# Which operand stands still: q/k/v, query and up products with stationary weights in a two-layer decoder trunk

## The chip, the core and the metric

The program runs on one core of a Trainium2 chip, in one launch, on fp32 inputs in device memory. The metric is the device time of one execution in microseconds (us), compared by the median of several runs. The engines are TensorE (PE in the profile; its weight loads have a row of their own, PEld), VectorE (DVE), ScalarE (ACT), GpSimd (POOL) and SyncE (SP), which issues the weight loads from device memory. Each engine takes its instructions in order from its own queue and waits for the others by semaphores. "The slices" are the profile's 40 equal parts of the span.

## The reference

Two layers over one sequence of 256 rows of 2048. Layer 0 is a gated DeltaNet, layer 1 a differential attention; each is followed by a squared-ReLU MLP of width 8192, and a LayerNorm closes every sub-layer.

```python
def gated_deltanet(x, w_in, ...):                    # w_in: 2048 x (q 2048 | k 2048 | v 2048 | z 2048 | 32)
    p = x @ w_in
    qkv = causal_conv_silu(p[..., :GDN_CONV_CH], conv_w)
    z = ...; beta = sigmoid(b); g = -exp(a_log) * softplus(a + dt_bias)
    # q, k normalised per head of 128; chunked delta rule with a triangular solve
    o = rms_norm(o, norm_w, GDN_EPS) * jax.nn.silu(z)
    return o @ w_out

def diff_attention(x, w_q, ...):                     # k, v = x @ w_kv
    attn = softmax(q1 k1) - lam * softmax(q2 k2)     # per head, causal
    return (rms_norm(attn @ v) * (1.0 - lambda_init)) @ w_o

def sq_relu_mlp(x, w_up, w_down):
    return jnp.square(jax.nn.relu(x @ w_up)) @ w_down

x = layer_norm(ALPHA * x + h, ln_g[l, 0], ln_b[l, 0])
x = layer_norm(ALPHA * x + sq_relu_mlp(x, mlp_w_up[l], mlp_w_down[l]), ln_g[l, 1], ln_b[l, 1])
```

## The kernel before

**Split products.** Every large product keeps fp32 accuracy by splitting both operands into two parts of the type fp32r: hi, a copy by ACT (L78), and lo, the rest, a subtraction by DVE (L79). A product is then x_hi W_hi + x_hi W_lo + x_lo W_hi, summed in PSUM. `xhl` holds both parts of x with features on the 128 partitions, as blocks of [part, row tile t, feature block k, 128 rows].

**A weight tile** is 128 input features by 1024 columns, 512 KB, loaded into `wr` by SP, and split into `wh` and `wl`. `product` (L166) runs 12 matmuls on it: for each of two row tiles t and two column halves g, with a 128x128 block of x as the stationary operand and 512 columns of the weights streaming past:

```python
mm(ps, xh, wh[:, c], start=(k == 0), stop=False)                      # L174
mm(ps, xh, wl[:, c], start=False, stop=False)                         # L175
self.last = mm(ps, xl, wh[:, c], start=False, stop=(k == nk - 1))     # L176
```

The result has rows on partitions, [128 rows, 512 columns], one PSUM bank for each (g, t): four accumulators `acc`, which a product of 1024 columns uses all. The other four banks, `ps`, serve everything else.

**The plan.** `gemm` puts a product on a list; `run` (L121) walks it in steps of four weight tiles (48 matmuls). A step is t = 0 for all tiles, then t = 1; the loads of the next step's tiles are written between the two. After each t, `pump(rate)` writes down the next units of other work: one from the deque `chain`, and up to `rate` from `units`. `soon` puts a function behind a tile of the next product. What is written down is what each engine's queue holds, in that order, save that TensorE's part of some functions is tied behind the last matmul so far.

**Back to features.** The next product needs its operand with features on partitions. So up products (`up`, L341) take relu and square, and then four 128x128 transpositions by TensorE (`transpose4`, L200; the matmuls stand at L204) and another split per accumulator. q, k and v of DeltaNet are copied out of `acc` by ACT (L693), transposed, and copied into a tile `raw` of [128 channels, 8 heads, 256 rows] (`channels`, L498). Differential queries and keys are turned the same way in `heads` (L787).

**DeltaNet's order.** It works in two halves of 8 heads. Each half's plan is k, q, v (1024 columns each, four steps), `rate=2`; z follows both halves. When a product is through, `follow` (L704) queues units: four conv units of two heads for k or q (`qk_unit`, L476: a causal convolution of four taps on DVE, L471, a tanh and a square on ACT, and sums of squares by matmuls of one column, L485), four `v_unit`s, and, after q, `scalars`, four `score` units (L513: masks on DVE, L525 and L526, decay matmuls at L530 to L535, k k and q k at L550 and L551, their weighting on DVE at L553 and L554) and the inverse, as a chain. The gate projection stands ahead of q of the first half (`gates`, L410): there the small weights are stationary, hi against hi and lo of x (512 columns, L425) and lo against x's hi (256 columns, L426).

**The start.** `load_x` (L226) loads x and splits it quarter by quarter, the first at once, the others as units between the steps of the first product.

In the differential part a `score` unit (L809) is one pair of heads and one row tile: matmuls (L819), a masked maximum on DVE (L830), four exponentials on ACT (L834), and the weighted difference.

## Time and profile before

| | |
|---|---|
| time, median of 3 runs | 2463.02 us (2461.49 to 2467.75) |
| the profiled execution | 2465.03 us, span 2463.3 us |
| granted TensorE clock, mean of the span | 0.992 |
| PE busy | 2416.1 us, 11492 matmuls |
| DVE busy | 1497.2 us, 2333 instructions |
| ACT busy | 1078.2 us, 1474 instructions |
| POOL busy | 90.3 us |
| matmuls at L174, L175, L176 with x as operand | 3 x 1920, with a mean of 393 to 398 ns |
| weight splits, L78 on ACT and L79 on DVE | 800 of 1052 ns, 785 of 1227 ns |

A matmul's row gives its own duration, from its start to its modelled end, and matmuls overlap: where they follow each other without a gap, the time that one costs is the distance from one start to the next. A row of a listing of instructions has its start (us from the start of the span), its duration (us), engine, line, operation, output and inputs, shapes, and in brackets, if it waited, how long and for what. A row of a group has the number of instructions, the busy time and the mean duration in ns, and the idle time before them.

### The profile page before, as it was taken

Reading aid. Unit: us, or ns where it says so; the run is one execution under the profiler, and the core shown is the slowest. Engines: PE = TensorE matmul, PEld = TensorE weight load, DVE = VectorE, ACT = ScalarE, POOL = GpSimd, SP = SyncE. Lnnn points to the kernel's source line nnn. Section 1 sums busy time; section 2 is a strip of 40 time slices with the busy share of each in tenths; the row PEclk is TensorE's granted clock in tenths of the full one; section 3 lists DMA queues with packets and bytes.
Section 4 is the critical chain, followed back from the end, with each engine's and each line's share of the span. In section 5 each row is a group of like instructions: output and inputs, shape, how many; then the busy total and the mean of one; then the engine's idle time right before and its main releaser. Section 6 shows DMA issues by size and latency. Waiting matters only on the chain.

```text
span 2463.3 us, 30465 instructions
## 1 busy us (share of the span) xinstructions
PE 2416.1 (98%) x11492; PEld 1983.3 (81%) x11492; DVE 1497.2 (61%) x2333; ACT 1078.2 (44%) x1474; POOL 90.3 (4%) x94
## 2 busy tenths in 40 slices
PE   8999999998999999999998999999999999999997
PEld 7888888887888888888887878788788888888886
DVE  4789689667554544545557575665755554555556
ACT  4545345433443433434433464643443443443442
POOL 0010010002000000000002000000200000000001
PEclk9999899999999999999999999999999999999999
DMA  6545345564555556565554545455455555656553
GB/s 229 155 139 175 98 140 160 166 233 158 188 185 191 182 194 222 172 214 182 195 197 146 180 137 171 155 174 167 161 198 195 182 190 186 217 179 214 185 195 121
DMA packets 120211, 438.84 MB, mean 178 GB/s; under 512 B 13760, under 2 KB 13792, under 8 KB 119040
## 3 DMA queue, kind: packets, MB, share of 16 engines
q1 hardware_dynamic: 115920, 420.79, 52.0%
q0 software_dynamic: 2560, 11.13, 1.4%
q10 hardware_dynamic: 1584, 4.98, 0.5%
q8 instruction: 90, 1.47, 0.2%
q14 instruction: 57, 0.47, 0.1%
HBM read 433.70 MB, written 3.15 MB: 177 GB/s over the span
## 4 chain that ended last, share of the span: by engine, by line
PE 90%; DVE 6%; DMA 2%; issue 1%; ACT 1%; POOL 0%; ACTq 0%; POOLq 0%; DVEq 0%
PE acc L174 27%; PE acc L175 27%; PE acc L176 27%; PE ps L204 3%; DVE wl L79 1%; DVE blk L266 1%; DVE blk L265 1%; PE ps L819 1%; ACT wh L78 1%; PE ps L550 1%; DMA wr<-in_gdn_w_in_dram 1%; PE ps L485 1%; DMA wr<-in_mlp_w_up_dram 0%; PE ps L621 0%; PE ps L847 0%
## 5 line engine op out<-in xcount | busy, mean ns | idle before, releaser
L79 DVE TENSOR_TENSOR wl<-wr,wh 128x1024 fp32r<-128x1024 f32 x785 | 954.5, 1227 | 675.0 <-ACT wh L78 632.1
L78 ACT CAST wh<-wr 128x1024 fp32r<-128x1024 f32 x800 | 832.1, 1052 | 945.6 <-PE acc L176 757.2
L174 PE MATMUL acc<-wh,xhl 128*128 128x512 f32 x1920 | 764.3, 398 | 0.0
L175 PE MATMUL acc<-wl,xhl 128*128 128x512 f32 x1920 | 757.7, 395 | 3.2 <-POOL wl L79 3.2
L176 PE MATMUL acc<-wh,xhl 128*128 128x512 f32 x1920 | 754.8, 393 | 0.0
L174 PE MATMUL acc<-wh,blk 128*128 128x512 f32 x1280 | 500.0, 391 | 0.0
L176 PE MATMUL acc<-wh,blk 128*128 128x512 f32 x1280 | 499.4, 390 | 0.0
L175 PE MATMUL acc<-wl,blk 128*128 128x512 f32 x1280 | 499.1, 390 | 0.0
L175 PEld LDWEIGHTS acc<-wl,xhl 128*128 128x128 f32 x1920 | 363.7, 189 | 75.7 <-POOL wl L79 4.4
L174 PEld LDWEIGHTS acc<-wh,xhl 128*128 128x128 f32 x1920 | 363.8, 189 | 73.8 <-issue 1.7
L176 PEld LDWEIGHTS acc<-wh,xhl 128*128 128x128 f32 x1920 | 362.7, 189 | 73.9
L176 PEld LDWEIGHTS acc<-wh,blk 128*128 128x128 f32 x1280 | 240.4, 188 | 50.1
L174 PEld LDWEIGHTS acc<-wh,blk 128*128 128x128 f32 x1280 | 240.4, 188 | 49.5
L175 PEld LDWEIGHTS acc<-wl,blk 128*128 128x128 f32 x1280 | 240.5, 188 | 49.2
L293 DVE SCALAR_TENSOR_TENSOR blk<-blk,acc 128x512 f32<-128x512 f32 x80 | 54.7, 685 | 85.2 <-PE acc L176 85.2
L204 PE MATMUL ps<-ident,sm 128*128 128x128 f32 x512 | 81.3, 275 | 2.5 <-DVE sm L869 1.8
L204 PEld LDWEIGHTS ps<-ident,sm 128*128 128x128 f32 x512 | 61.3, 140 | 27.3 <-PE acc L176 7.1
L78 ACT CAST blk<-ps 128x512 fp32r<-128x512 f32 x80 | 46.8, 585 | 70.9 <-PE ps L204 70.9
L347 DVE TENSOR_TENSOR sm<-sm 128x512 f32<-128x512 f32 x64 | 44.0, 691 | 52.6 <-ACT sm L346 52.2
L79 DVE TENSOR_TENSOR blk<-ps,blk 128x512 fp32r<-128x512 f32 x80 | 55.0, 688 | 30.1 <-ACT blk L78 30.1
L346 ACT ACTIVATE sm<-acc 128x512 f32<-128x512 f32 x64 | 38.2, 597 | 65.4 <-PE acc L176 62.4
L471 DVE SCALAR_TENSOR_TENSOR sm<-blk,g_cw,sm 128x255 f32<-128x255 f32 (+2 forms) x144 | 60.8, 474 | 0.0
(202 smaller groups left out, 1049.7 us busy)
## 6 DMA issues: line engine op xcount, KB each, us to landing
wr<-in_mlp_w_up_dram SPq DMA_DIRECT2D x256, 512.0 KB, 4.7
wr<-in_mlp_w_down_dram SPq DMA_DIRECT2D x256, 512.0 KB, 5.2
wr<-in_gdn_w_in_dram SPq DMA_DIRECT2D x128, 512.0 KB, 4.4
wr<-in_shared_w_kv_dram SPq DMA_DIRECT2D x64, 512.0 KB, 5.1
wr<-in_gdn_w_out_dram SPq DMA_DIRECT2D x32, 512.0 KB, 5.4
wr<-in_diff_w_q_dram SPq DMA_DIRECT2D x32, 512.0 KB, 4.6
wr<-in_diff_w_o_dram SPq DMA_DIRECT2D x32, 512.0 KB, 4.7
blk<-in_ln_g_dram POOLq DMA_DIRECT2D x4, 1024.0 KB, 7.2
```

The lines of the kernel that those rows point to most:

```text
L78: self.nc.scalar.copy(hi, src)
L79: (engine or self.nc.vector).tensor_tensor(lo, src, hi.bitcast(F32), op=ALU.subtract)
L174: mm(ps, xh, wh[:, c], start=(k == 0), stop=False)
L175: mm(ps, xh, wl[:, c], start=False, stop=False)
L176: self.last = mm(ps, xl, wh[:, c], start=False, stop=(k == nk - 1))
L204: self.nc.tensor.transpose(pt[:, i], src[:, i * P : (i + 1) * P], self.ident)
L265: v.scalar_tensor_tensor(xc, xc, ln["mv", t][:, 0:1], ln["g"][:, c], op0=ALU.subtract, op1=ALU.mult)
L266: v.scalar_tensor_tensor(xc, xc, ln["rs", t], ln["b"][:, c], op0=ALU.mult, op1=ALU.add)
L293: self.nc.vector.scalar_tensor_tensor(rc, rc, alpha, ps, op0=ALU.mult, op1=ALU.add)
L346: self.nc.scalar.activation(a, ps, AF.Relu)
L347: self.nc.vector.tensor_tensor(a, a, a, op=ALU.mult)
L471: v_.scalar_tensor_tensor(y[:, i, d:], u[:, : T - d], w(j), y[:, i, d:], op0=ALU.mult, op1=ALU.add)
```

## The change

In the products q, k and v of DeltaNet, the queries and the second half of the keys of the differential part, and all up products but the first 1024 columns of each layer's, the weights become the stationary operand, and the result comes out with features on partitions. The list of the plan gets a second kind of entry (`features`), of 512 columns; a step has again four weight tiles of 512 KB, each now two blocks of 128 input features by 512 columns, in pieces of 2 KB per row in place of 4 KB.

For each input block k and each block b of 128 output features, `feature_passes` runs two matmuls into one PSUM bank: W_hi stationary against hi and lo of x in one pass of 512 columns, and W_lo against x's hi in one of 256. So the bank holds hi terms in its left half and W_hi x_lo in its right. `joined` brings them together: ACT copies the right half out, DVE adds the left. To let hi and lo of x stand next to each other, `xhl` and the MLP's activations become [k, part, 256 rows].

PSUM is cut differently: `acc` is now two tiles of two banks, and a new product uses both. The transpositions of these results go, with their copies; relu, square and split of up work on two tiles of 512. Half a step is four input blocks with all four b (32 matmuls); in the first half step the passes go through b 0 and 1 first, in the last through one b after the other. The loads of the next step and one pump stand behind the first half step, another pump behind the second, as before; the evacuation is written behind the last pass, ahead of that pump.

z, down, the output products, the differential values, and the first product behind each MLP-side LayerNorm (keys, first half; up, first 1024 columns) stay as they were.

```diff
-        self.acc = pool("acc", 4, space=PSUM)
+        self.acc = pool("acc", 2, space=PSUM)
...
-        self.xhl = self.const.tile([P, 2, NT, KD, P], F32R, name="xhl")
+        self.xhl = self.const.tile([P, KD, 2, T], F32R, name="xhl")
...
+    def features(self, w, c0, evac, pre=None, rate=1):
+        wsrc = lambda k: w[k * P : (k + 2) * P, c0 : c0 + G].rearrange("(k p) c -> p k c", p=P)
+        self.plan.append((KD, wsrc, None, evac, pre, rate, None, [2 * SC] * (KD // (2 * SC))))
...
+            if stat is None:
+                if s == 0:
+                    acc = [self.acc.tile([P, NG, G], F32, name="acc") for _ in range(2)]
+                self.feature_passes(acc, ws, evac if s + n >= nk else None, lambda: self.load_next(loaded, steps, j), rate)
+                continue
...
+    def load_next(self, loaded, steps, j):
+        if j + 1 < len(steps):
+            with self.after(self.hold):
+                self.load_weights(loaded, *steps[j + 1], self.hold is not None)
+            self.hold = None
...
+    def feature_passes(self, acc, ws, evac, load, rate):
+        mm = self.nc.tensor.matmul
+        def passes(kn, b):
+            k0, wh, wl = ws[kn // 2]
+            k, c = k0 + kn % 2, slice(kn % 2 * G + b * P, kn % 2 * G + (b + 1) * P)
+            ps = acc[b // 2][:, b % 2]
+            mm(ps, wh[:, c], self.xhl[:, k], start=(k == 0), stop=False, skip_group_check=True)
+            self.last = mm(
+                ps[:, :T], wl[:, c], self.xhl[:, k, 0], start=False, stop=(k == KD - 1), skip_group_check=True
+            )
+        half = len(ws)
+        for n, ks in enumerate((range(half), range(half, 2 * half))):
+            if ws[0][0] == 0 and n == 0:
+                order = [(k, b) for bb in (0, 2) for k in ks for b in (bb, bb + 1)]
+            elif evac is not None and n == 1:
+                order = [(k, b) for b in range(4) for k in ks]
+            else:
+                order = [(k, b) for k in ks for b in range(4)]
+            for m, (k, b) in enumerate(order):
+                passes(k, b)
+                if m % 4 == 3 and m + n > 3 and self.pending:
+                    fn, args = self.pending.popleft()
+                    with self.after(self.last):
+                        fn(*args)
+            if n == 0:
+                load()
+                self.pump(rate)
+        if evac is not None:
+            evac(acc)
+        self.pump(rate)
+    def joined(self, pair, dst=None):
+        t = self.sm().rearrange("p (b t) -> p b t", b=2)
+        self.nc.scalar.copy(t, pair[:, :, T:])
+        self.nc.vector.tensor_tensor(t if dst is None else dst, pair[:, :, :T], t, op=ALU.add)
+        return t
...
+        for k in range(s, s + n, 2 if pairs else 1):
             wr = self.raw.tile([P, C], F32, name="wr")
-            self.nc.sync.dma_start(wr, wsrc(k))
+            self.nc.sync.dma_start(wr.rearrange("p (k c) -> p k c", k=2) if pairs else wr, wsrc(k))
...
+            def up_features(blocks, h=h):
+                h.append(self.blk(F32R))
+                hv = self.act_view(h[-1])
+                a = [self.joined(blocks[i]) for i in range(2)]
+                for i in range(2):
+                    self.nc.scalar.activation(a[i], a[i], AF.Relu)
+                for i in range(2):
+                    self.nc.vector.tensor_tensor(a[i], a[i], a[i], op=ALU.mult)
+                for i in range(2):
+                    kb = slice(2 * i, 2 * i + 2)
+                    self.split(hv[:, kb, 0], hv[:, kb, 1], a[i])
...
+            first = C if f == 0 else 0
+            if first:
+                self.gemm(KD, self.cols(w_up, 0), self.x_stat, up(0), cuts=[6, 5, 5])
+            for c0 in range(first, FQ, G):
+                self.features(w_up, f * FQ + c0, up_features)
...
-                    if (gi, t) == (0, 0):
+            def ev_for(name, ct, u):
+                def ev(blocks):
+                    if u == 0:
                         hf["raw"] = self.blk().rearrange("p (h t) -> p h t", h=HH)
-                    a = self.sm()
-                    nc.scalar.copy(a, ps)
-                    if (gi, t) == (NG - 1, NT - 1):
-                        turned(gi, t, a)
-                    else:
-                        self.soon(turned, gi, t, a)
-
-                def turned(gi, t, a):
-                    channels(a, gi, t, hf["raw"])
-                    if (gi, t) == (NG - 1, NT - 1):
+                    for h in (0, 2):
+                        self.joined(blocks[h // 2], hf["raw"][:, u * 4 + h : u * 4 + h + 2])
+                    if u == 1:
                         follow()
...
-                self.gemm(KD, self.cols(w_in, c0 + H * DK), self.x_stat, ev_for(name, ct + H), pre=pre, rate=2)
+                for u in range(2):
+                    self.features(
+                        w_in, c0 + H * DK + u * G, ev_for(name, ct + H, u), pre=pre if u == 0 else None, rate=2
+                    )
...
+        def head_features(name, u, follow=None):
+            def ev(blocks):
+                if u == 0:
+                    st[name] = self.blk().rearrange("p (h t) -> p h t", h=8)
+                for h in (0, 2):
+                    self.joined(blocks[h // 2], st[name][:, u * 4 + h : u * 4 + h + 2])
...
+            for u in range(2):
+                self.features(w_q, hh * C + u * G, head_features("q", u, follow))
...
+            if hh == 0:
+                self.gemm(KD, self.cols(w_kv, 0), self.x_stat, heads("k"), pre=constants, cuts=[6, 5, 5])
+            else:
+                for u in range(2):
+                    self.features(w_kv, C + u * G, head_features("k", u))
+            q_heads(hh)
```

What moves on the engines' queues is shown at three places. In these rows the letters stand for line, operation, output<-inputs with buffer numbers, shape.

**First place: TensorE, first half of DeltaNet, where v's second part begins.** Before, v was one product with four accumulators (`acc_1046` and `acc_1050` for the first row tile, `acc_1134` and `acc_1138` for the second); its passes lay around the matmuls of each score, here of the second (L530 to L551):

```order
L174 MATMUL acc_1050<-wh_1284,xhl_89 128x512
L175 MATMUL acc_1050<-wl_1285,xhl_89 128x512
L176 MATMUL acc_1050<-wh_1284,xhl_89 128x512
L174 MATMUL acc_1134<-wh_1266,xhl_89 128x512
...
L175 MATMUL acc_1134<-wl_1273,xhl_89 128x512
L530 MATMUL ps_1299<-sm_1288,g_after_112 128x512
L534 MATMUL ps_1300<-sm_1290,g_after_112 128x256
...
L551 MATMUL ps_1324<-blk_1006,blk_524 128x128
L176 MATMUL acc_1134<-wh_1272,xhl_89 128x512
```

After the change the first 512 columns of v end in `acc_1135`; then come the norm of the last conv unit and three scores' matmuls, and only then the second 512 columns, in `acc_1572`:

```order
L184 MATMUL acc_1135<-xhl_89,wl_1189 128x256
L563 MATMUL ps_1224<-g_col1_114,sm_1222 128x1 x4
L605 MATMUL ps_1308<-sm_1297,g_after_112 128x512
...
L605 MATMUL ps_1409<-sm_1398,g_after_112 128x512
...
L605 MATMUL ps_1454<-sm_1443,g_after_112 128x512
...
L626 MATMUL ps_1479<-blk_1094,blk_568 128x128
L183 MATMUL acc_1572<-xhl_89,wh_1376 128x512
```

The passes that used to lie between score matmuls now stand in front of and behind a group of them.

**Second place: DVE at the same point.** Before, the third score's weightings (L553, L554) were followed by the next score's masks, with no work on `acc`:

```order
L553 SCALAR_TENSOR_TENSOR blk_1193<-ps_1368,g_c_1173,sm_1352 128x256
L554 SCALAR_TENSOR_TENSOR blk_1194<-ps_1369,g_c_1173,sm_1353 128x128
L525 TENSOR_SCALAR sm_1402<-mask_90,g_g_117 128x256
```

After the change the two additions (L213) that empty v's accumulators stand between them (the weightings are now L628 and L629):

```order
L628 SCALAR_TENSOR_TENSOR blk_1295<-ps_1478,g_c_1275,sm_1462 128x256
L629 SCALAR_TENSOR_TENSOR blk_1296<-ps_1479,g_c_1275,sm_1463 128x128
L213 TENSOR_TENSOR blk_1520<-acc_1134,sm_1521 128x512
L213 TENSOR_TENSOR blk_1520<-acc_1135,sm_1524 128x512
L600 TENSOR_SCALAR sm_1527<-mask_90,g_g_117 128x256
```

So DVE comes to the additions when it is through with the weightings in front of them.

**Third place: TensorE in the first product (k).** The transpositions `ps_203` to `ps_250` make x's second and third quarter out of the rows (`blk_92`, `blk_93`). Before, between two quarters lay the passes of the first quarter with the second row tile:

```order
L176 MATMUL acc_157<-wh_139,xhl_89 128x512
L204 MATMUL ps_203<-ident_84,blk_92 128x128 x4
L204 MATMUL ps_210<-ident_84,blk_93 128x128 x4
L176 MATMUL acc_217<-wh_121,xhl_89 128x512
L175 MATMUL acc_221<-wl_122,xhl_89 128x512
...
L176 MATMUL acc_221<-wh_139,xhl_89 128x512
L204 MATMUL ps_243<-ident_84,blk_92 128x128 x4
L204 MATMUL ps_250<-ident_84,blk_93 128x128 x4
L174 MATMUL acc_153<-wh_181,xhl_89 128x512
```

Now the passes of the new quarter stand right behind its transpositions:

```order
L184 MATMUL acc_154<-xhl_89,wl_128 128x256
L267 MATMUL ps_211<-ident_84,blk_92 128x128 x4
L267 MATMUL ps_218<-ident_84,blk_93 128x128 x4
L183 MATMUL acc_153<-xhl_89,wh_133 128x512
L184 MATMUL acc_153<-xhl_89,wl_134 128x256
```

Both row tiles of a quarter are now wanted at once, half a step after the quarter before.

54 lines of the change are left out of this document (21 added, 33 removed).

## The prediction

> **What bounds the kernel now.** I read the page first: busy shares, the 40 slices, the chain that ended last.
>
> ```profile
> PE 2416.1 (98%) x11492; PEld 1983.3 (81%) x11492; DVE 1497.2 (61%) x2333; ACT 1078.2 (44%) x1474; POOL 90.3 (4%) x94
> PE   8999999998999999999998999999999999999997
> DVE  4789689667554544545557575665755554555556
> PE 90%; DVE 6%; DMA 2%; issue 1%; ACT 1%; POOL 0%; ACTq 0%; POOLq 0%; DVEq 0%
> ```
>
> TensorE holds 90% of the chain and hardly rests in any slice, so whatever it no longer issues is time won, and whatever makes it wait is time lost. VectorE (DVE) has room on average, but not in slices 1 to 8, the DeltaNet stage. Then I read windows of single stages:
>
> ```profile
> 118.00:165.20 47.20, 47.20 (x243) 39.61 (x243) 43.33 (x112) 20.59 (x29) 2.37 (x6) 1.00 0.51 156
> 183.00:206.00 23.00, 22.98 (x110) 18.12 (x108) 22.96 (x58) 14.48 (x27) 0.00 (x0) 1.00 0.47 152
> 230.00:262.30 32.30, 31.96 (x162) 26.05 (x161) 29.06 (x63) 15.75 (x21) 3.17 (x5) 1.00 0.59 164
> 310.70:358.00 47.30, 47.30 (x244) 39.71 (x243) 43.38 (x112) 20.62 (x29) 2.40 (x6) 1.00 0.50 155
> 700.00:800.00 100.00, 100.00 (x443) 82.88 (x442) 50.31 (x46) 38.92 (x38) 0.00 (x0) 1.00 0.57 190
> ```
>
> The columns are length, then busy time (and instructions) of PE, PEld, DVE, ACT, POOL, then granted clock, DMA share, GB/s. The last row is a stretch of MLP products only: 443 matmuls, two of them cut by the edges, in 100 us, 0.2268 us for a pass of 512 columns, with DVE half idle. The rows at 118 and 310.7 are the v products of the two DeltaNet halves: DVE is busy for 43.3 of 47 us. Today TensorE needs nothing there from DVE but the lo parts of weights, which run ahead.
>
> **The transposes that go.** A transposition of 128x512 is four matmuls; one in an up product of the last MLP:
>
> ```profile
> 2310.60 0.39 PE L176 MATMUL acc<-wh,xhl 128*128 128x512 f32 x1
> 2310.83 0.60 PE L204 MATMUL ps<-ident,sm 128*128 128x128 f32 x4
> 2311.18 0.48 PE L174 MATMUL acc<-wh,xhl 128*128 128x512 f32 x1
> 2311.50 0.39 PE L175 MATMUL acc<-wl,xhl 128*128 128x512 f32 x1
> 2311.73 0.39 PE L176 MATMUL acc<-wh,xhl 128*128 128x512 f32 x1
> ```
>
> From 2310.60 to 2311.73 are 1.13 us with three passes of 512 in them (0.68), so the four cost 0.45. The up products lose 56 such groups (64, less the 8 of the two products that stay as they were), DeltaNet's q, k and v lose 24, the differential queries 8 and the keys' second half 4: 92 x 0.45 = **-41.4 us**.
>
> **The passes that are cut differently.** Per weight tile, before: 12 passes of 512 columns, 12 x 0.2268 = 2.72 us. After: 8 pairs of 512 and 256, the same 6144 columns in 16 matmuls, each with its own weight load. The gate projection has run just this alternation all along:
>
> ```profile
> 82.56 0.28 PE L426 MATMUL ps<-xhl,blk 128*128 128x256 f32 x1
> 82.68 0.40 PE L425 MATMUL ps<-xhl,blk 128*128 128x512 f32 x1
> 82.91 0.28 PE L426 MATMUL ps<-xhl,blk 128*128 128x256 f32 x1
> ...
> 87.86 0.28 PE L426 MATMUL ps<-xhl,blk 128*128 128x256 f32 x1
> 87.98 0.40 PE L174 MATMUL acc<-wh,xhl 128*128 128x512 f32 x1
> ```
>
> From 82.56 to 87.86 are 15 pairs in 5.30 us: 0.353 each, 0.0128 more than 1.5 x 0.2268. Tiles of the new kind (issue rows):
>
> ```profile
> wr<-in_mlp_w_up_dram SPq DMA_DIRECT2D x256, 512.0 KB, 4.7
> wr<-in_gdn_w_in_dram SPq DMA_DIRECT2D x128, 512.0 KB, 4.4
> ```
>
> Of up 256 - 32 = 224, of w_in 128 - 32 (z) = 96, of w_q 32, of w_kv 16: 368 tiles, 2944 pairs, x 0.0128 = **+37.7 us**. From below: a pass of 256 alone takes 0.117 (87.86 to 87.98), so an undisturbed pair is 0.344 and the term 0.0038 x 2944 = +11. I take 0.353: it is the same alternation. The gates read x in strided pieces of 128 and the new code reads 512 in one run, which is what could make it cheaper.
>
> [...]
>
> **The accumulators that DVE now empties.** This is the largest term. Before, an accumulator of q, k or v was free after one copy by ACT. Now there are two accumulators of two banks, a product uses both, and each is free only after ACT's copy and DVE's addition. DVE's queue is in order: the addition stands behind all units of conv and scores that were issued earlier, and TensorE's next product stands behind the addition. So the idle time is the end of that DVE work less TensorE's own work up to there. Behind the waiting pass stand the other passes of its product; they free the weight buffers, so ACT's casts and SP's loads come late with it and cost nothing more.
>
> v, both halves. Before, from q's last copy to the third score's last write:
>
> ```profile
> 117.95 0.59 ACT L693 COPY sm<-acc 128x512 f32<-128x512 f32 x1
> 165.24 0.34 DVE L554 SCALAR_TENSOR_TENSOR blk<-ps,g_c,sm 128x128 f32<-128x128 f32 x1
> L174 PE MATMUL acc<-wh,xhl 128*128 128x512 f32 x47 | 18.6, 397 | 0.0
> 67.93 1.02 PE L485 MATMUL ps<-g_col,sm 128*128 128x1 f32 x8
> 68.81 0.48 PE L176 MATMUL acc<-wh,xhl 128*128 128x512 f32 x1
> ```
>
> (The third row is the window 118:165.2; L175 and L176 have 47 there too.) That is 47.6 us, with DVE nearly full. The first v product's addition now stands right behind this third score, with two weight subtractions fewer and four additions more ahead of it, which cancel. TensorE in that time: 64 pairs, 22.6; four norm groups at 0.88 (67.93 to 68.81), 3.5; and the three scores. These are what is left of 47.2 when 141 passes (32.0), the norms (3.5) and one transposition (0.45) are taken out: 11.2. Idle 47.6 - 37.3 = 10, twice: **+20**.
>
> q of the first half, behind the gate computation and two conv units:
>
> ```profile
> 88.58 0.42 DVE L429 TENSOR_TENSOR sm<-ps,sm 128x256 f32<-128x256 f32 x1 [3.62 <-ACT sm L428]
> 106.74 0.16 DVE L486 TENSOR_SCALAR g_Sk<-ps 128x4 f32<-128x4 f32 x1
> L79 DVE TENSOR_TENSOR wl<-wr,wh 128x1024 fp32r<-128x1024 f32 x7 | 8.5, 1220 | 0.1
> L347 DVE TENSOR_TENSOR sm<-sm 128x512 f32<-128x512 f32 x64 | 44.0, 691 | 52.6 <-ACT sm L346 52.2
> ```
>
> From the gates' last matmul to the second unit's end 18.3 us, less five of the seven subtractions (6), plus a copy (0.59) and an addition (priced as the 128x512 of L347, 0.69): 13.6. TensorE still has 13 matmuls (2.3) and two norm groups (1.8): **+10** (9.5).
>
> The first k product of half two has the four conv units of v ahead of it (183:206, 23 us all busy, two subtractions and two additions more: 27) against 22.6 + 1.9 for the v transposes: **+2**. The first q product of half two: 32.3 us at 230:262.3, against 22.6 + 3.5: at least **+5**. Elsewhere in DeltaNet DVE has less to do than TensorE's 22.6. Together **+37 us**, from half of it (DVE packed closer than before) to 60 (units that wait for each other when nothing fills the gaps).
>
> TensorE comes back slow from such a rest. At the start it ran so:
>
> ```profile
> 11.02 0.79 PE L174 MATMUL acc<-wh,xhl 128*128 128x512 f32 x1
> 15.02 0.56 PE L174 MATMUL acc<-wh,xhl 128*128 128x512 f32 x1
> ```
>
> Nine passes lie from the one to the other, in 4.0 us where 2.04 would do: about half speed, 1.9 us lost. After three rests of 10 us: **+5.7** (0 if the scores' matmuls keep the clock up). [...]
>
> **The first 40 us.** x's features come in four quarters, and the new product asks for a quarter half a step after the one before (the third place above). Behind the end of a half step come one weight cast whose buffer is only then free, its subtraction, and two splits of x:
>
> ```profile
> 19.97 1.07 ACT L78 CAST xhl<-ps 128x512 fp32r<-128x512 f32 x2 [0.30 <-PE ps L204]
> 20.85 1.28 DVE L79 TENSOR_TENSOR xhl<-ps,xhl 128x512 fp32r<-128x512 f32 x2
> 22.48 1.05 ACT L78 CAST wh<-wr 128x1024 fp32r<-128x1024 f32 x1 [0.33 <-PE acc L176]
> 25.01 1.03 PE L204 MATMUL ps<-ident,blk 128*128 128x128 f32 x8
> 25.80 0.48 PE L174 MATMUL acc<-wh,xhl 128*128 128x512 f32 x1
> ```
>
> Cast 1.05 + subtraction 1.22 + splits 1.28 = 3.55, of which the transposes (25.01 to 25.80) cover 0.8: a wait of 2.8, three times: **+8.4 us**. Before, the 24 passes of the second row tile stood there and covered it.
>
> **The rest.** In the differential part, two key products' additions stand behind a score unit whose exponentials alone take four of these:
>
> ```profile
> L834 ACT ACTIVATE sm<-sm,m 128x128 f32<-128x128 f32 (+1 forms) x64 | 28.5, 446 | 30.1 <-DVE m L830 30.0
> ```
>
> I take **+4** (0 to 8). In the MLPs the new copy and addition, 1.3 us a pair, lie in ACT and DVE time that is half free; the second pair is released 2.35 us after the last pass (a cast ends 0.4 after it, subtraction 1.22, addition 0.69) and needed after 8 pairs, 2.8: nothing, with 0.45 to spare. Pieces of 2 KB instead of 4 in the loads: nothing, since a tile lands in under 5 us and is used a step (11 us) later.
>
> **Sum.** 2465.0 (the profiled execution, span 2463.3) - 41.4 + 37.7 + 8.4 + 37 + 5.7 + 4 = 2516.4; this execution stood 2.0 above the median, so **2514 us**, 2.1% slower.
>
> **Rivals.**
> 1. *The passes are cheap, the waits are as said*: 0.344 a pair, 2514 - 26 = 2488. For it, the contiguous read; against it, that what sets the gate passes off from the plain stream is above all the alternation, and that stays.
> 2. *DVE never holds an accumulator*, because units run early enough, and passes are cheap: 2463 - 41 + 11 + 8 = 2441, **faster**. It decides once DVE's work ahead of an addition is under TensorE's 22.6 to 37 us. Against it, 43.3 of 47.2 us busy and an order in which the additions stand last.
> 3. *No waits, passes as in the gates*: 2463 - 41 + 38 + 8 = 2468, no change.
> 4. *The MLP's 0.45 us is not there either*: 28 products lose about 1 us each, 2514 + 28 = 2542. For it, the tight count; against, a DVE half idle there.
>
> **How the numbers follow.** Forecast 0.60, rival 1 0.13, rival 2 0.08, rival 3 0.07, rival 4 0.12. The range leaves rival 2 out: low 2466 (half of the waits, cheap passes, or rival 3), high 2552 (waits of 60 and some of rival 4). About 0.3%, 7 us, is what a measurement tells from none: faster 0.08, same 0.07, slower 0.85.
>
> **What would show it.** Pairs of 353 ns at the new matmul lines; L204 down by 368; in DeltaNet two rests of TensorE of about 10 us in front of the second v product of each half, and one behind the gates, released by DVE's addition; three of 2.8 us in the first 45; the MLP stretches within 2 us a stage. I am wrong in the mechanism if TensorE has no rests over 5 us between 60 and 360, and in the size if the pair is 344.

## The result

The changed kernel takes 2547.47 us (median of 4 runs, 2544.10 to 2552.40) against 2465.39 us before (4 runs): a ratio of 1.0323, with a 95% interval of 1.0276 to 1.0370. The profiled execution took 2547.13 us, 82 more than the one before; the forecast was 51 more. The page of the changed kernel (busy times, the slices that answer to those shown before, with the granted clock as a last row, and the chain by engine):

```profile
PE 2439.3 (96%) x12596; PEld 2043.7 (80%) x12596; DVE 1544.6 (61%) x2413; ACT 1093.3 (43%) x1506; POOL 88.0 (3%) x94
PE   6898998999999999999999999999899999999997
DVE  3667856955755554554556665666755554554656
PEclk8899888999999999999999999999999999999999
PE 77%; issue 10%; DVE 7%; DMA 2%; ACT 1%; POOL 0%; ACTq 0%; POOLq 0%; SPq 0%; DVEq 0%
```

The clock row before:

```profile
PEclk9999899999999999999999999999999999999999
```

TensorE rests more and runs slower in the first seven slices; behind them the rows differ by hardly a digit. DVE's share is what it was. How late each product ends against before says where the 82 us arise. The table is worked out from the starts of the products' last matmuls in both traces; a column is what was added between the end of the product ahead and its own, in us, also where the next product's first passes lie among its last (k, q, v of the first half are k0, q0, v0; "out" is DeltaNet's output product; "rest" is all that follows it, up to the last down product).

| kernel | k0 | q0 | v0 | k1 | q1 | v1 | z0 | z1 | out | rest |
|---|---|---|---|---|---|---|---|---|---|---|
| changed | +18.2 | +13.5 | +13.9 | +3.9 | +7.6 | +15.7 | -0.7 | +8.8 | +4.0 | -2.8 |

DeltaNet with its output product holds 84.9 us; both MLPs and the differential part together come out 2.8 us ahead. An up stage of one layer's second quarter and later (four products of 512 columns) is the cleanest view of the passes. The third one of the first MLP, before and then after (columns as in the windows above):

```profile
946.50:1037.00 90.50, 90.50 (x414) 74.69 (x413) 48.53 (x48) 41.15 (x47) 0.56 (x1) 1.00 0.59 198
```

```profile
1033.00:1123.00 90.00, 90.00 (x510) 77.89 (x509) 53.75 (x55) 45.11 (x54) 0.00 (x0) 1.00 0.64 199
```

Same length within half a microsecond, no rest in either, and DVE and ACT are still free for 40% and 50% of it. In the last MLP's rows of the changed kernel the pair itself can be read:

```profile
2400.12 0.40 PE L183 MATMUL acc<-xhl,wh 128*128 128x512 f32 x1
2400.35 0.28 PE L184 MATMUL acc<-xhl,wl 128*128 128x256 f32 x1
2400.47 0.39 PE L183 MATMUL acc<-xhl,wh 128*128 128x512 f32 x1
...
2401.51 0.40 PE L183 MATMUL acc<-xhl,wh 128*128 128x512 f32 x1
```

From 2400.12 to 2401.51 are four pairs: 0.348 each, in the least disturbed stretches; over all 2944 pairs the median is 0.350. Transpositions saved and pairs dearer than 1.5 passes cancel, as the two terms of the sum said they would.

**Inside DeltaNet.** TensorE's waits between 60 and 480 us (engine, what it was about to run, what released it: total us, times, longest):

```profile
PE ps L563 <- ACT sm L557: 20.0, 6, 6.0
PE ps L605 <- DVE sm L600: 7.9, 4, 2.2
PE acc L183 <- DVE blk L213: 7.2, 3, 3.0
PE ps L605 <- DVE rsq_t L89: 2.5, 2, 1.2
...
```

Before, the same view from 60 to 420 us (z's first product ends at 422 there, at 494 here) held no more than this:

```profile
PE ps L204 <- DVE sm L739: 0.5, 1, 0.5
PE ps L485 <- ACT sm L479: 0.3, 1, 0.3
```

Only 7.2 us end with the addition that empties an accumulator (L213); most end with a unit's own small matmul. The timeline of the longest place, where v's first 512 columns end and its second begin, shows why:

```profile
173.33 0.28 PE L184 MATMUL acc<-xhl,wl 128*128 128x256 f32 x1
...
175.97 1.53 PE L563 MATMUL ps<-g_col,sm 128*128 128x1 f32 x8 [2.37 <-ACT sm L557]
...
187.19 0.50 PE L605 MATMUL ps<-sm,g_after 128*128 128x512 f32 x1 [2.16 <-DVE sm L600]
...
193.09 0.52 PE L605 MATMUL ps<-sm,g_after 128*128 128x512 f32 x1 [1.89 <-DVE sm L600]
...
196.80 1.08 ACT L212 COPY sm<-acc 128x512 f32<-128x512 f32 x2
...
197.15 0.48 DVE L628 SCALAR_TENSOR_TENSOR blk<-ps,g_c,sm 128x256 f32<-128x256 f32 x1 [3.01 <-POOL sm L616]
...
199.76 1.28 DVE L213 TENSOR_TENSOR blk<-acc,sm 128x512 f32<-128x512 f32 x2
200.50 0.50 PE L183 MATMUL acc<-xhl,wh 128*128 128x512 f32 x1 [1.97 <-DVE blk L213]
```

For 27 us TensorE has no pass of a product. One unit after another goes round from DVE's masks over TensorE, ACT, POOL and back to DVE, 6 to 8 us each, and with no passes to fill in, every engine waits for the next. The additions come behind the third unit, the next product behind them. ACT's copy (L212) is as late as DVE's addition: it too stands behind the unit's exponentials, and even DVE waits here (3.01 us for POOL).

**The start and the clock.** The window from 20 to 57 us, before and then after, and the rows of the changed kernel at the first pass and at the second quarter of x:

```profile
20.00:57.00 37.00, 37.00 (x176) 30.59 (x175) 19.50 (x20) 17.34 (x21) 0.00 (x0) 1.00 0.63 209
```

```profile
20.00:57.00 37.00, 28.19 (x137) 24.02 (x136) 13.48 (x16) 10.47 (x15) 0.66 (x1) 0.82 0.43 136
```

```profile
10.99 1.04 ACT L79 CAST wh<-wr 128x1024 fp32r<-128x1024 f32 x1 [4.18 <-DMA wr<-in_gdn_w_in_dram]
11.94 1.06 ACT L79 CAST xhl<-ps 128x512 fp32r<-128x512 f32 x2
...
14.55 0.79 PE L183 MATMUL acc<-xhl,wh 128*128 128x512 f32 x1 [4.32 <-DVE xhl L80]
...
24.75 1.06 ACT L79 CAST xhl<-ps 128x512 fp32r<-128x512 f32 x2
...
26.02 1.28 DVE L80 TENSOR_TENSOR xhl<-ps,xhl 128x512 fp32r<-128x512 f32 x2
...
27.36 0.80 PE L183 MATMUL acc<-xhl,wh 128*128 128x512 f32 x1 [3.92 <-DVE xhl L80]
28.16 0.63 PE L183 MATMUL acc<-xhl,wh 128*128 128x512 f32 x1
...
32.64 0.57 PE L183 MATMUL acc<-xhl,wh 128*128 128x512 f32 x1
```

The rests at the three later quarters are 3.92, 2.60 and 2.29 us. The first pass starts at 14.55 instead of 11.02: it needs hi and lo of both row tiles, where the first pass before needed hi of one, and ACT's casts of x stand behind the cast of a weight tile that landed late (the 4.18 us). That landing is not the same in every execution: with TensorE kept at work (below), where nothing ahead of the first pass is changed, it started at 16.41. From 28.16 to 32.64 seven pairs take 0.64 each, near twice 0.35: 2.0 us lost in those alone, more in those around them. Over the span the clock is granted at half for 118 us after the change and for 44 before. Each interval from one matmul's start to the next was sorted by its size and the granted clock: over the span they hold 65 us more of rest than before, 25 us more of slow passes, and 7 us less of other work.

### The profile page after: what moved, and what is told of

Its sections match the earlier page's. It is cut to its first block, busy times and chain, and to the rows that moved or that the text cites. A ratio compares the mean times of both kernels' runs of the same rounds, so it can differ in the third digit from the quotient of the medians.

```text
span 2545.4 us, 32691 instructions
## 1 busy us (share of the span) xinstructions
PE 2439.3 (96%) x12596; PEld 2043.7 (80%) x12596; DVE 1544.6 (61%) x2413; ACT 1093.3 (43%) x1506; POOL 88.0 (3%) x94
## 4 chain that ended last, share of the span: by engine, by line
PE 77%; issue 10%; DVE 7%; DMA 2%; ACT 1%; POOL 0%; ACTq 0%; POOLq 0%; SPq 0%; DVEq 0%
PE acc L183 22%; PE acc L237 13%; PE acc L239 13%; PE acc L238 13%; PE acc L184 11%; DVE wl L80 2%; PE ps L267 1%; ACT wh L79 1%; PE ps L903 1%; DVE blk L330 1%; DVE sm L549 1%; DMA wr<-in_mlp_w_up_dram 0%; DVE blk L662 0%; DVE sm L655 0%; DMA wr<-in_gdn_w_out_dram 0%
## 5 line engine op out<-in xcount | busy, mean ns | idle before, releaser
L183 PE MATMUL acc<-xhl,wh 128*128 128x512 f32 x2944 | 1053.3, 401 | 21.5 <-DVE xhl L80 13.1
L184 PE MATMUL acc<-xhl,wl 128*128 128x256 f32 x2944 | 833.3, 283 | 0.0
L183 PEld LDWEIGHTS acc<-xhl,wh 128*128 128x128 f32 x2944 | 560.5, 190 | 156.9 <-DVE xhl L80 14.1
L184 PEld LDWEIGHTS acc<-xhl,wl 128*128 128x128 f32 x2944 | 563.1, 191 | 2.3 <-issue 0.7
L238 PE MATMUL acc<-wl,xhl 128*128 128x512 f32 x448 | 178.8, 399 | 4.7 <-POOL wl L80 2.4
L237 PE MATMUL acc<-wh,xhl 128*128 128x512 f32 x448 | 179.8, 402 | 0.8 <-ACT wh L79 0.4
L239 PE MATMUL acc<-wh,xhl 128*128 128x512 f32 x448 | 178.4, 398 | 0.0
L238 PEld LDWEIGHTS acc<-wl,xhl 128*128 128x128 f32 x448 | 85.1, 190 | 24.4 <-POOL wl L80 4.5
L237 PEld LDWEIGHTS acc<-wh,xhl 128*128 128x128 f32 x448 | 85.3, 190 | 21.0 <-ACT wh L79 2.0
L239 PEld LDWEIGHTS acc<-wh,xhl 128*128 128x128 f32 x448 | 85.2, 190 | 17.7 <-DVE xhl L80 0.4
L212 ACT COPY sm<-acc 128x512 f32<-128x512 f32 x92 | 53.0, 582 | 74.7 <-PE acc L184 74.5
L213 DVE TENSOR_TENSOR sm<-acc,sm 128x512 f32<-128x512 f32 x56 | 38.5, 687 | 32.6 <-ACT sm L212 32.6
```

The costliest lines, as they stand in the source:

```text
L183: mm(ps, wh[:, c], self.xhl[:, k], start=(k == 0), stop=False, skip_group_check=True)
L184: self.last = mm(ps[:, :T], wl[:, c], self.xhl[:, k, 0], start=False, stop=(k == KD - 1), skip_group_check=True)
L212: self.nc.scalar.copy(t, pair[:, :, T:])
L213: self.nc.vector.tensor_tensor(t if dst is None else dst, pair[:, :, :T], t, op=ALU.add)
```

## The experiments

All times are device us; where there were several rounds, the ratio to the kernel before on the same chip is given with its 95% interval, since the kernel before itself gave medians from 2461 to 2471 in these sets. A kernel without a ratio was run once. The table of lateness, as above, for those that bear on DeltaNet; a row is one execution, and what the clock did in that one is in it (in q1, z0 and z1 up to 10 us, see the last section):

| kernel | k0 | q0 | v0 | k1 | q1 | v1 | z0 | z1 | out | rest |
|---|---|---|---|---|---|---|---|---|---|---|
| changed | +18.2 | +13.5 | +13.9 | +3.9 | +7.6 | +15.7 | -0.7 | +8.8 | +4.0 | -2.8 |
| old q, k, v | +1.0 | +0.3 | +0.2 | 0.0 | +1.3 | +0.2 | +1.0 | +8.8 | +3.8 | -5.3 |
| ACT frees | +18.2 | +11.3 | +10.0 | +0.1 | +12.5 | +9.8 | -1.2 | +17.1 | +3.8 | -3.0 |
| three passes | +13.0 | +0.9 | +0.9 | +0.7 | -1.7 | +0.5 | +0.3 | +2.4 | +1.5 | +15.8 |
| three, old k0 | +1.1 | +3.5 | +0.7 | +2.8 | -1.7 | +0.5 | +1.7 | +9.8 | +0.2 | +16.9 |
| old k0 | +1.4 | +14.4 | +15.0 | +4.9 | +7.8 | +12.7 | -1.2 | +9.6 | +3.4 | +2.8 |
| narrow, old k0 | +1.5 | +10.1 | +8.5 | -1.3 | -22.6 | +8.7 | +21.2 | +31.0 | +6.8 | +1.7 |
| one unit a time | +17.1 | +14.1 | +3.2 | +2.6 | -11.3 | +45.4 | +3.1 | +23.0 | +6.6 | +1.3 |
| all, single banks | +19.2 | +13.0 | +15.0 | +2.3 | +10.8 | +14.1 | -1.2 | +4.1 | 0.0 | -1.0 |
| old q, k, v, single banks | +0.9 | 0.0 | 0.0 | 0.0 | -8.6 | 0.0 | -0.5 | +2.1 | 0.0 | 0.0 |

**Old q, k and v in DeltaNet.**

```diff
-                for u in range(2):
-                    self.features(w_in, c0 + H * DK + u * G, ev_for(name, ct + H, u), ...)
+                self.gemm(KD, self.cols(w_in, c0 + H * DK), self.x_stat, ev_rows, pre=pre, rate=2)
```

> DeltaNet's q, k and v go back to x as the stationary operand (with their transpositions and one copy by ACT); up, the queries and the second half of the keys keep stationary weights, and the accumulators stay two tiles of two banks. Theory A (rests of TensorE in DeltaNet, where DVE empties both accumulators behind the units written earlier, with the slow clock behind each rest): all of the loss is in DeltaNet and its tail, so 2460 us, 2452 to 2468. Rival B (the new passes, loads of 2 KB pieces or longer evacuations cost wherever they stand): 272 of 368 new tiles stay, so 82 x 272/368 = 61 us stay, 2526. Rival C (the tail in z and the output product comes from accumulators that are freed two banks at a time): 13 us stay, 2478.

Measured: 2473.77, ratio 1.0047 (1.0032 to 1.0062), 12.8 us above the kernel before on the same chip. The general rival (2526) falls: the new passes and loads cost nothing in 272 of 368 tiles. But 12.6 us stay in z1 and the output product, where no pass had been changed. Rival C named that, and the runs with single banks take it up.

**The passes grouped.**

```diff
-                passes(k, b)
+                if m % 4 == 3:
+                    for lo in range(2):
+                        for k_, b_ in order[m - 3 : m + 1]:
+                            passes(k_, b_, lo)
```

> Of each input block the four passes of 512 columns come first and then the four of 256, in place of taking turns; all else is the changed kernel. If taking turns sets the pair's 350 ns, the pair falls to 340 to 344 (1.5 x 227, or 227 + 117) and the time by 18 to 29 us, to 2518 to 2529. If the weight load of each pass sets it, or if the 512 pass behind a 256 pass is what costs, a smaller share comes back: 2540 to 2547.

Measured: 2545.11, ratio 1.0340 (1.0324 to 1.0355); the changed kernel's was 1.0323 (1.0276 to 1.0370): no difference that can be told. In the trace an up stage of 256 pairs is 0.7 us shorter than in the changed kernel, 0.0027 a pair. So taking turns is not what sets the pair's price: most of it stays when four of a kind follow each other. It sits in the pass of 512 columns: with weights stationary its median from start to start is 0.232 us when taking turns and 0.234 in groups, where passes with x stationary have 0.227 in the same traces. Why is open.

**Three passes of 256 columns.** x's hi and lo add into the same columns, so an evacuation is a copy by ACT, and a product holds one accumulator tile of two.

```diff
-            mm(ps, wh[:, c], self.xhl[:, k], start=(k == 0), ...)
-            self.last = mm(ps[:, :T], wl[:, c], self.xhl[:, k, 0], ...)
+            ps = acc[:, b]
+            mm(ps, wh[:, c], self.xhl[:, k, 0], start=(k == 0), ...)
+            mm(ps, wh[:, c], self.xhl[:, k, 1], ...)
+            self.last = mm(ps, wl[:, c], self.xhl[:, k, 0], ...)
-        self.nc.vector.tensor_tensor(t if dst is None else dst, pair[:, :, :T], t, op=ALU.add)
+        self.nc.scalar.copy(dst, pair)
```

> The pass of 512 columns (x hi and lo at once) is cut in two of 256 that add into the same place: W_hi on x hi, W_hi on x lo, W_lo on x hi, each of 256 columns. So no addition by DVE is left, a product takes one tile of two banks, and the next one has the other. Theory A: TensorE's passes cost 3 x 0.117 = 0.351 a block against 0.350 for the pair, the rests at DVE's additions and most of the cold clock go (about 43 + 15 us), the first 60 us stay as they are: 2474 to 2495. Rival B: 2540 to 2550. If the passes of 256 back to back cost more than 0.117 because of the three weight loads: above 2550.

Measured: 2499.98, ratio 1.0151 (1.0128 to 1.0174). In this kernel each block's first pass carries the start bit, also the second block's in a bank, and its sums are not whole: the result is off by 0.346 (relative), where the kernel with the bit set once a bank (below) gives the whole sum. Every pass is still run, so its time is that of the whole work. DeltaNet from q0 to v1, in the window of its trace and TensorE's waits between 60 and 400 us:

```profile
75.00:388.00 313.00, 312.18 (x2590) 304.65 (x2590) 250.89 (x628) 134.25 (x212) 25.47 (x43) 0.97 0.48 140
```

```profile
PE ps L263 <- DVE sm L548: 1.3, 2, 1.0
PE ps L499 <- ACT blk L79: 0.3, 1, 0.3
```

TensorE is busy for 312.18 of 313 us, and the five products add 1.3 us in place of 54.6. So the rests come from the way a product's result leaves the accumulators, not from the passes. The time is 5 us above the upper end for this case, because a pass of 256 among its like costs 0.120, not 0.117: three cost 0.360, and the rest of the program is 15.8 us late instead of 2.8 early.

**ACT copies both halves out**, DVE adds in SBUF.

```diff
-        self.nc.vector.tensor_tensor(t if dst is None else dst, pair[:, :, :T], t, op=ALU.add)
+        self.nc.scalar.copy(dst, pair[:, :, :T])
+        self.nc.vector.tensor_tensor(dst, dst, t, op=ALU.add)
```

> Where the result goes to q, k, v or the differential heads, ACT copies both halves out of the accumulator and DVE adds them in SBUF, so that the accumulator no longer waits for DVE. If the addition itself holds the accumulator (theory A in its narrow form), the rests in front of the second v product shrink by several us each and the time falls by 20 to 40 us, to 2507 to 2527. If what holds it is the place of the whole evacuation behind the units written earlier (their exponentials on ACT, their tiles of the sm pool), less than 8 us comes back: 2540 to 2547.

Measured: 2543.58, the end that was written for "the place of the whole evacuation". Through v1 it is 10.8 us earlier than the changed kernel (62.0 late, not 72.8), of which z1 gives 8.3 back. TensorE's waits are of the same kind (23.1 us for a unit's squares, 8.1 for its masks), and from 60 to 480 us they fall only from 39.0 to 35.2. The 8.3 in z1 are not the edit's: in this one execution the clock was at half for 20.5 us there with TensorE busy throughout. That the addition is DVE's is a small part; that the evacuation, on whichever engine, stands behind the units is the larger.

**The old k product at the start.**

```diff
+                if hh == 0 and name == "k":
+                    self.gemm(KD, self.cols(w_in, c0 + H * DK), self.x_stat, ev_rows, pre=pre, rate=2)
+                    continue
```

> The changed kernel with the first half's k product as before (x stationary). If the 18 us of the first 80 us come from x's quarters, wanted for both row tiles at once, they go, and nothing else moves: 2529 to 2533. If the first product's lateness had covered work of DVE that now stands in q's way: 2540 to 2547.

Measured: 2535.90 in one run, between the two. The first product's 18.2 us go (+1.4), and q0, v0 and k1 add 3 us more than in the changed kernel. At the end of the output product 16.8 us are won, so the start is a cost of its own; later stages, in which nothing differs, gave 5.6 of it back in this run.

**TensorE kept at work at the start**, with six groups of transpositions behind each later quarter.

```diff
                 self.to_features(r[t][:, cut(q)], self.xhl[:, q * 4 : q * 4 + 4], t)
+                if q and t:
+                    for _ in range(6):
+                        self.transpose4(r[t][:, cut(q)])
```

> The changed kernel, with six groups of four transpositions that nobody reads behind those of each later quarter of x, about 2.6 us of TensorE at full clock, in front of the rests of 4.7, 4.1 and 2.8 us. If a rest over some 3 us brings the slow clock, the rests shrink below that, the half-clock windows at 26, 40 and 50 us go, and the first product ends about 5 us earlier: 2542. If the slow clock has another cause, or the transpositions themselves run slow and delay the passes, the windows stay and the time is 2547 or more.

Measured: 2547.21 in one run. The window of this kernel's trace that answers to the one of the start above:

```profile
20.00:57.00 37.00, 36.98 (x240) 32.68 (x240) 16.64 (x19) 12.83 (x17) 1.21 (x1) 1.00 0.49 149
```

The clock is 1.00 in place of 0.82, and the first product ends 4.1 us earlier although 72 transpositions were added and its first pass came 1.9 later. The transpositions filled the rests, and the slow clock went with them. So at this start rests of 2.3 to 3.9 us (the trace's; the expectation had put them at 2.8 to 4.7) brought the slow clock, and work that nobody needs avoided both. The whole program did not become shorter: up to the output product it was 5.3 us ahead of the changed kernel, and the later stages (no part of them was edited) lost it again. One run leaves open whether that is more than scatter.

**Narrow products.** As with the old k, but q, k and v come in products of 256 columns with one accumulator tile each.

```diff
-                for u in range(2):
-                    self.features(w_in, c0 + H * DK + u * G, ..., rate=2)
+                for u in range(4):
+                    self.narrow(w_in, c0 + H * DK + u * T, ..., rate=4)     # one pump behind each product
```

> As k0_old, but DeltaNet's q, k and v are cut into products of 256 columns (four input blocks in a weight tile, pieces of 1 KB), each with one accumulator of two banks, so that the next product has the other while this one is emptied by ACT's copy and DVE's addition, as changed. If the rests come from a product that holds both accumulators until its evacuation is through, they mostly go although DVE's additions stay: 2475 to 2495. If DVE's additional work or its order is what TensorE waits for in any case: 2520 to 2533. If pieces of 1 KB load too slowly, waits for wr by DMA appear in the rows of ACT's casts.

Measured: 2530.38, between the two. It was a poor test, for it also writes units four at a time and the inverse's steps half as often, so that work moved to z (+21.2 and +31.0). Where only q0 and v0 had run, its lateness grew by 18.6 us against 29.4 with the old k alone: with another tile free, a third of that went although DVE's additions stayed. TensorE's longest waits there are again for a unit's squares (8.6 us in two, against 11.6 in three).

**One unit in place of two** behind each half step.

```diff
-                        w_in, c0 + H * DK + u * G, ..., rate=2
+                        w_in, c0 + H * DK + u * G, ..., rate=2 if hh == 0 and name == "k" else 1
```

> The changed kernel with one unit in place of two written behind each half step in DeltaNet (the first product keeps two, for x's quarters). If the rest is the DVE work written ahead of an evacuation, half of the units stand there, the rests of 27 us in front of the second v products shrink to less than half, and 15 to 30 us come back, of which the units that move into z may take some: 2517 to 2535. If the place of the units does not matter: 2547.

Measured: 2569.96, slower, which neither theory had. v0 does shrink from 13.9 to 3.2, as the place of the units has it. But the units that were put off pile up with the inverse and the solves in v1 (+45.4) and z1 (+23.0), where TensorE waits for them in the same way.

**Accumulators of one bank again**, first with the old q, k and v, then in the changed kernel.

```diff
-        self.acc = pool("acc", 2, space=PSUM)
+        self.acc = pool("acc", 4, space=PSUM)
...
-            if k == 0 and g == 0:
-                pair = self.acc.tile([P, NG, G], F32, name="acc")
-                acc.update({(i, t): pair[:, i] for i in range(NG)})
+            if k == 0:
+                acc[g, t] = self.acc.tile([P, G], F32, name="acc")
```

> As up_only (q, k and v of DeltaNet with x stationary; up, queries and second keys with stationary weights), but with four accumulators of one bank again: a new product takes all four, and each is copied and added by itself. If the 12.7 us up to the end of z, the 3.8 in the output product and the 0.7 of each down product come from accumulators that are freed two banks at a time, they go: 2461 - 8 (up and the differential part) + 3 = 2456, 2452 to 2461. If they come from the new layout of x and the activations, or from another order of the queues, the time stays at 2470 to 2476.

Measured: 2461.02, ratio 0.9985 (0.9963 to 1.0008), against 1.0047 with two banks at a time: the first reading. The longest waits of z1 and the output product, with two banks at a time (425 to 600 us) and with one (415 to 576):

```profile
PE ps L267 <- DVE rsq_t L88: 3.0, 1, 3.0
PE acc L238 <- DVE wl L80: 3.0, 1, 3.0
PE ps L692 <- DMA blk<-g_inverses: 2.4, 1, 2.4
...
```

```profile
PE ps L693 <- DMA blk<-g_inverses: 2.3, 1, 2.3
```

All but the last of these waits are gone, z1 and the output product fall from +12.6 to +2.1, and a down stage is 0.6 us faster than before where it had been 0.7 slower (the up stage ahead of it, 0.8 ahead with two banks, is level here).

> The changed kernel with four accumulators of one bank in place of two of two banks; everything else as changed. Singles against up_only showed some 13 us for this in products that kept x stationary (z, output, down). If that part is additive to the rests in q, k and v: 2547 - 13 to 18 = 2529 to 2534. If the rests in q, k and v come from freeing two banks at a time as well: below 2515. If it only counted beside the old q, k and v: 2540 to 2547.

Measured: 2541.34, ratio 1.0283 (1.0240 to 1.0326): 6 us less than the changed kernel, not 13 to 18, and the two intervals overlap. By the rows, z1 and the output product fall from 12.8 to 4.1, but q0 to v1 stay (55.2 against 54.6): the rests in q, k and v do not come from the size of an accumulator. The price that was taken over from the pair of kernels with the old q, k and v was too high, for 9.9 us of it had arisen in q1 (-8.6 against +1.3), where the last section finds the clock.

**Single banks, old q, k and v, grouped passes.**

> As singles, with the four passes of 512 columns of an input block ahead of its four of 256. Grouping took 0.7 us more off each up stage in the changed kernel: 5 us less than singles, 2451. If single accumulators change how the passes meet the evacuations, the same as singles, 2456.

Measured: 2460.21, ratio 0.9966 (0.9947 to 0.9985): 0.3%, 8 us, below the kernel before on the same chip. Against the kernel without grouping (0.9985) the intervals overlap. Executions of this set with the same granted clock, 0.994, say more: 2449.6 to 2453.3 here, 2453.4 and 2456.6 without grouping, 2458.5 to 2460.9 before. In the profiled execution 14.2 us were won: 5.9 behind the output product, where up and the differential part have stationary weights, and 8.3 ahead of it, nearly all in q1, where no product is changed and the clock alone differs (last section).

> As the kernel with three passes of 256 columns, but k of the first half is the old product again, and only the first block of a bank has the start bit. If the 13 us that the three-pass kernel is late at the end of its first product come from x's quarters, which are wanted for both row tiles at once, they go: 2487, 2482 to 2492. If the lateness only moves on to q (its conv units and the gates stand behind the same weights), 2496 to 2502.

With the start bit set once a bank and the old k: 2494.90, ratio 1.0116 (1.0087 to 1.0144), in us between what the two readings gave. As a ratio to the 2461 us on which the readings were built, the first one's 2482 to 2492 are 1.0085 to 1.0126, and the measured ratio lies inside. By the rows the first product's 13.0 us fall to 1.1 and q0 takes 3.5. z1's 9.8 come in the main from the clock: the profiled execution, the longest of the four, has half clock for 17.1 us there, and the one without the old k has none.

## Why the forecast held, and where it fell short

The direction and the places were right: two long rests in front of v's second parts, one behind the gates, three at the start, MLPs even. The measured 82 us are 31 more than the 51 forecast, though inside the range. That it lies inside is in part luck: the upper end was set for longer waits and some of rival 4, and the excess came in the main from slow passes (15.5 more than forecast) and from z and the output product (12.8, forecast at nothing).

- **Transpositions and passes.** Right: the two terms nearly cancel. By them an up stage of four new products (8 groups of transpositions, 256 pairs) changes by -8 x 0.45 + 256 x 0.0128 = -0.3; measured -0.8 in five of the six that have four, and -2.4 in the sixth. The pair is 0.350, nearer to the gates' 0.353 than to 0.344. Rival 1 (cheap passes) falls. The reason given, that the alternation sets the price, is not borne out: grouping took off 0.0027 of the 0.010 by which a pair is dearer than 1.5 passes.
- **Accumulators.** The term was 37, and the rests from q0 to v1 measure 43 more than before. v, both halves: 10 forecast each, 10.6 and 10.4 measured; q0 9.5 against 11.8; k1 2 against 3.0; q1 5 against 7.1. The mechanism was too narrow. It said that TensorE stands behind the addition because DVE's queue is in order, in rests of about 10 us that DVE's addition ends. The longest single wait is 6.0 us, and those that end with the addition are 7.2 together; with the accumulator freed by ACT most of the rest stayed. That the sizes agree so closely, with another engine's work ending most of the waits, is in part luck. What held in every run with such products: a product that takes all accumulators leaves TensorE nothing but units to run until the evacuation's turn has come on ACT and DVE, and the units then run at the pace of their own round trip.
- **The slow clock.** 5.7 forecast behind three rests of 10; measured 15.4 from q0 to v1 and 5.8 at the start. Two things were missed: the long rests are chains of shorter ones with small matmuls in between, in part at half clock, and rests of 2 to 4 us cost it too. The sum had slow passes behind the rests of 10 us alone and none behind those of 2 to 5, which was wrong here: at the rests of 3.92, 2.60 and 2.29 us the trace has half clock for 6.8, 3.4 and 3.4 us.
- **The start.** 8.4 forecast, 18.2 measured: 8.8 in the three rests, as the term had it, 3.5 in front of the first pass, which waits for hi and lo of both row tiles (the term left that out; with TensorE kept at work it was 1.9 more), and 5.8 of slow passes (it left those out as well).
- **z and the output product.** The sum had nothing here; 12.8 measured. It is the step that gave every product the same PSUM, two tiles of two banks, at no cost: a product with x stationary had been able to take a bank as soon as it was free. Where DVE and ACT run late, as at the end of z1, that one bank mattered. Single banks brought 8.7 of the 12.8 back.
- **The MLP's 0.45 us.** There, as forecast. Rival 4 came nearest in its total (2542), by a mechanism that the up stages exclude. The differential part's +4 did not appear: keys, queries and values ended 2.1 us earlier than before, relative to the stage ahead. Up to 3.4 of that is the clock, which in the profiled execution before was at half for 3.4 us twice in this part, and after the change not at all.

Open: how much of what the three passes bring is the second tile and how much the absence of DVE's addition. The narrow products were meant to tell and changed the units' order as well. Open too is why a pass of 512 columns with stationary weights is dearer.

## What to carry to other kernels

Before a product's result takes a second engine to leave PSUM, look at what stands ahead of that evacuation in both queues, and at what the next product needs to start: it is the time from the last pass to the evacuation's turn, less the time for which another accumulator keeps TensorE busy. Where the change also alters how PSUM is cut, products that were not touched can pay as well (here 12.6 us in z1 and the output product with the old q, k and v), so time it in them apart. And price a rest of TensorE with the slow passes behind it: here 65 us of rests came with 25 us of slow passes.

## What the runs showed of the hardware

- **Half clock without a rest.** In the kernel before, in q1, TensorE is busy all the time, and yet the clock falls to half for 20.5 us. First its rows, then the window behind them:

```profile
264.57 1.10 PE L621 MATMUL ps<-blk,sm 32*32 32x32 f32 x29
...
265.60 0.98 PE L628 MATMUL ps<-sm,blk 32*32 32x32 f32 x26
266.51 1.08 PE L617 MATMUL ps<-blk 32*32 32x32 f32 x29
267.52 0.50 PE L176 MATMUL acc<-wh,xhl 128*128 128x512 f32 x1
```

```profile
268.00:288.00 20.00, 20.00 (x126) 15.92 (x125) 5.63 (x6) 5.09 (x7) 0.00 (x0) 0.50 0.31 91
```

Three microseconds of matmuls of 32x32, with hardly a pass between, stand ahead of it. In the kernel with single banks and the old q, k and v the window reads 1.00:

```profile
268.00:288.00 20.00, 20.00 (x212) 16.79 (x209) 9.16 (x24) 8.82 (x25) 0.00 (x0) 1.00 0.40 130
```

That is its 8.6 us in q1. Yet TensorE's matmuls come in the same order there, 1.3 us later: a group of 32x32, five passes, three groups of 32x32, four passes. What differs is where the clock's steps lie. In the traces of the kernel before (5 stretches) and of the changed kernel (17) a stretch of half clock lasts 3.41 us or a whole multiple of it (but for the ones in which the program ends, 12.86 and 12.45 us), and within each of the two traces the starts of these stretches lie whole multiples of 3.41 us apart; the first starts at 267.95 us before and at 26.19 after, so the origins differ. The step of 3.41 us ahead of the fall in the kernel before, and then the steps that hold the same matmuls with single banks:

```profile
264.54:267.95 3.41, 3.41 (x99) 3.29 (x99) 2.59 (x4) 0.32 (x1) 0.00 (x0) 1.00 0.94 298
```

```profile
264.37:267.78 3.41, 3.41 (x77) 2.88 (x75) 3.37 (x4) 0.58 (x1) 0.00 (x0) 1.00 0.79 262
267.78:271.19 3.41, 3.41 (x77) 2.88 (x74) 0.73 (x2) 1.62 (x2) 0.00 (x0) 1.00 0.80 309
```

The first has passes only in its last 0.4 us; of the others one holds five passes and the next four. So this gain may hang on where the steps fell in one execution, and is not shown to be the kernel's. That the small matmuls are the cause is an inference; no run varied them alone. With the old q, k and v and two banks at a time the gain is not there: q1 has +1.3, and the clock from 60 to 376 us is 0.96, where the kernel before has 0.97 from 60 to 375.

- **The rests at the start** fit the same steps. The three stretches of half clock there begin at 26.19, 39.84 and 50.08 us, and TensorE rests for 2.3 to 2.8 us of the 3.41 ahead of each.

- **Passes of 256 columns** cost 0.117 when they take turns with passes of 512, and 0.120 among their like, where 512 columns cost 0.227 with x stationary and, with the weights stationary, 0.232 in turns and 0.234 in groups (medians): half the columns are about half the time, with a weight load each.
